# A two-layer hybrid trunk whose instruction order comes from a list scheduler: the same work placed by the finer of its two machine models

## The chip, the cores and the metric

One core of one Trainium2 chip runs the whole program in one launch. The metric is device time in microseconds (us): median of the runs, lower is better. Each of the core's engines works through its own list of instructions in the order in which the list stands: PE (matmul, with its weight loads shown apart as PEld), DVE, ACT and POOL (elementwise work) and SP (issues the DMAs). Engines wait for each other by semaphores. The order of every list is fixed when the program is built, and that order is all that this case changes.

## The reference, cut to what matters

Two layers over 1024 latent tokens and 256 context tokens, 1024 features, all in fp32:

```python
for l in range(DEPTH):                                    # DEPTH = 2
    h_lat = rms_norm(x, g_attn_pre[l]) * (1 + sc1) + sh1   # sh, sc, gt: 6 vectors from adaln(c)
    h_ctx = rms_norm(ctx, g_attn_pre[l]) * (1 + csc1) + csh1
    y_lat, y_ctx = hybrid_mixer(h_lat, h_ctx, ...)
    x = x + gt1 * rms_norm(y_lat, g_attn_post[l])
    h = rms_norm(x, g_mlp_pre[l]) * (1 + sc2) + sh2
    x = x + gt2 * rms_norm(square(relu(h @ w1)) @ w2, g_mlp_post[l])
    ...                                                    # the same for ctx, but in the last layer

def hybrid_mixer(h_lat, h_ctx, ...):
    p = h @ w_in                        # ONE projection, 24 tiles of 128 columns
    # 4 heads of gated DeltaNet: chunks of tokens, a triangular solve in each chunk,
    # then a scan over the chunks, forwards and backwards: S <- S * g + k^T (u - w S)
    # RG-LRU: gates, then a linear recurrence over the tokens, both directions
    # latent attention: 4 heads, keys and queries from small latents, softmax(q k^T) v
    return concat([gdn, rglru, mla]) @ w_out
```

## The kernel before, in words

Activations lie feature-major, 128 features on the partitions and tokens along the row; the tokens are three blocks, "c" (256) and two latent blocks of 512. A large product runs in three passes over operands split into a high and a low part (`mm3`, L222): for each of 8 feature tiles, two matmuls with the high weights `wh` and one with the low weights `wl`. So a tile of 128 output features and 512 tokens is 24 matmuls of 512 columns. The elementwise helpers put nearly all their instructions on four lines: L134 (ACT), L137 (two-operand work on DVE or POOL), L142/L143 (one operand) and L146 (DVE).

In each layer comes first the mixer, then the output projection, then the MLP. The mixer has four kinds of work, and the whole case turns on how they lie beside each other:

- **Projections.** The 24 tiles of `w_in`, each with an evacuation from PSUM and, for most, a short convolution (L146 on DVE) and an activation.
- **Heads.** Four DeltaNet heads (`gdn_head`), one after the other, since the large tiles of a head (`kT`, `qT`, `vt`, `N0`, `at0`, `C`, `X`, ...) have one buffer each. A head is a chain: decays and products of its chunks (L606, L618, L628), the triangular solve, which begins with 30 steps of two DVE instructions (`T<-X`, `X<-X,T`, L137, called from `gdn_invert`) and goes on with small matmuls (L678), then the scan: 10 steps in each direction, and in each step a matmul from the state (L748), one with the inverse (L752), one into the next state (L762) and the outputs (L771, L772), with a DVE or ACT instruction between one and the next. At the end come the norm and transposes of its output (L803).
- **RG-LRU.** 20 segments (`segment` in `lru`): four small matmuls (L830), some ten ACT, ten DVE and nine POOL instructions each, on tiles called `lr`.
- **Attention.** For each of 4 heads a preparation (L934, L942, the maxima L968, L974, L981) and the attention itself (scores L998 to L1000, exponentials on ACT, products with the values L1013). The steps of the adaLN vectors (L258) are mixed into it in layer 0. After it the output projection begins.

In the program's text the order is: the projection tiles of heads 0 to 2, each followed by its head; the two RG-LRU inputs; the tiles of head 3 and head 3; the attention's latents; then RG-LRU and attention. RG-LRU and attention take the memory of the projection's input (`close(self.ap)`), so they can't start before the projections have ended.

Nobody writes the order of the engines by hand. Tile's list scheduler runs the program through a model of the machine in time. Whenever an engine of the model can take an instruction, it gets the one of highest priority (earliest in the program's text, but for a few shifted by `later`) among those whose inputs and buffers are there in the model's time. What the model believes of durations and queues therefore decides which instruction is ready when, and that decides the order that the chip then keeps to.

Of the kernel before, what the change touches and what calls it, by code (L numbers as in the profile page):

```python
# [17 lines left out]
D = 1024  # L18
# [10 lines left out]
# token blocks in the joined order [context | latent]: (start, length)  # L29
# [4 lines left out]
# columns of the per-layer table of small parameters  # L34
# [9 lines left out]
class Trunk:  # L44
# [35 lines left out]
    @contextmanager  # L80
    def actor(self, name, t, g):
        """scratch of its own for a stream of work that runs beside others: t = (pool, buffers), g = PSUM tags."""
        old, self.cur = self.cur, (name, t, g)
        yield
        self.cur = old

    @contextmanager
    def later(self, n=0):
        """work beside what follows it: it takes no place in the order of the engines, and stands n steps later in it"""
# [6 lines left out]
    def T(self, half=None):  # L96
        name, (pool, bufs), _ = self.cur
        if name == "s":
            # two tags, so that a phase can keep two streams apart
            self.ht = 1 - self.ht if half is None else half  # L100
            name, bufs = "s%d" % self.ht, bufs // 2
# [22 lines left out]
    def M4(self, n):  # L124
        """PSUM for the products of a phase that leaves most banks free"""
# [22 lines left out]
    def split(self, dst, src, eng=None):  # L148
        """dst[:, 0] + dst[:, 1] = src, each part of few enough bits for one pass."""
# [12 lines left out]
    def softplus(self, out, x, tmp):  # L162
        """out = max(x, 0) + log1p(exp(-|x|)); tmp(): scratch of x's shape."""
# [15 lines left out]
    def rstd_bc(self, s, n, dim, eps=EPS):  # L179
        """s [128, n] (to be summed over partitions) -> PSUM [128, n]: rsqrt(sum / dim + eps) on every partition."""  # L180
# [13 lines left out]
    def sqsum(self, s, x, first, eng=None):  # L194
        """s (+)= x * x"""
# [20 lines left out]
    def mm3(self, ps, w, acts, ks):  # L216
        """ps = sum over ks of w[k]^T @ acts, in three passes of the split operands."""
# [17 lines left out]
    def ada_mods(self, L, v):  # L235
        """the vector v of (shift, scale, gate) x 2 is there: the products with the gains"""
# [8 lines left out]
    def ada_pe(self, L, vs, pool, tag, bufs, ptag):  # L245
        """one or two vectors of the modulation of a layer, for both streams, by TensorE: a list of steps"""
# [31 lines left out]
    def ada_steps(self, L, vs):  # L278
        """other vectors of the modulation, by VectorE, a quarter of a vector at a time: a list of steps"""
# [27 lines left out]
    def tick(self, n):  # L307
        """n steps of the work that is spread between the weights"""
# [9 lines left out]
    def prenorm(self, b, xs, s, L, which):  # L318
        """xs: 8 fp32 [128, n], s: sum of their squares (None: already normalised) -> 8 split tiles of the
        modulated norm; overwrites xs"""  # L320
# [19 lines left out]
    def fetch(self, src, b, pool, tag, bufs):  # L340
        """x of a block, two feature tiles in one buffer -> 8 tiles"""
# [8 lines left out]
    def post(self, b, ys, s, L, which, xs, xdst, want_sq=True):  # L350
        """ys <- x + gate * norm(ys); written to xdst; returns the sum of squares of the new x."""
# [30 lines left out]
    def conv_tile(self, L, hs, i, col, blocks, done, bias=None):  # L382
        """one projected tile -> depthwise convolution over each segment -> done(block, result)."""
# [22 lines left out]
    def silu2(self, acc):  # L406
        """acc <- 2 silu(acc)"""
# [5 lines left out]
    def qk_tile(self, L, hs, i, ct, blocks, name, tok=False):  # L413
        """-> 2 silu(conv), feature-major (and token-major), and the sums of its squares, a column for each chunk"""
# [20 lines left out]
    def v_tile(self, L, hs, i, ct, blocks, name):  # L435
        """values, token-major"""
# [14 lines left out]
    def z_tile(self, L, hs, i, blocks, d):  # L451
        """silu(z) times the gain of the head norm"""
# [9 lines left out]
    def gelu_tile(self, L, hs, i, blocks, d):  # L462

        def evac(b, ps):
            # gelu(g) = g (1 + tanh(sqrt(2/pi) (g + 0.044715 g^3))) / 2
# [15 lines left out]
    def kv_tile(self, L, hs, i, name):  # L481
        """normalised key/value latents"""
# [12 lines left out]
    def cq_tiles(self, L, hs, i, blocks, name):  # L495
        """normalised query latents: two tiles with one norm"""
# [26 lines left out]
    def gdn_coeffs(self, L, ba):  # L523
        """ba [128, NCH, 16] token-major -> decay and beta columns."""
# [48 lines left out]
    def gdn_head(self, L, h, kss, qss, vd, last):  # L573
        """The keys stay without their l2 norm 1 / rho: with D = diag(rho), the triangular system is solved as
# [815 lines left out]
```

## Time and profile before

| | |
|---|---|
| runs (us) | 3942.18, 3945.51, 3947.01: median 3945.51 |
| span of the profiled execution | 3934.6 us |
| that execution's own time | not listed apart; the median run is 10.9 us above the span |
| PE busy | 3567.8 us, 91% |
| DVE, ACT, POOL busy | 57%, 38%, 30% |
| mean granted PE clock | 0.948 |

Times below are microseconds from the start of the span. By the trace layer 0's mixer lasts to about 1009, its output projection and MLP to about 2190, layer 1's mixer from there to 3039, and the rest is its output projection and MLP. A row of a stretch (as "237.00:366.00") gives for PE, PEld, DVE, ACT and POOL the busy time and, in brackets, the number of instructions, then the granted PE clock (1.00 is full), the share of the DMA engines and their GB/s. PE counts as busy from a matmul's start to its modelled end, and matmuls overlap, so a PE that is busy all the time need not be at its peak. An fp32 matmul that isn't split is two records in the trace and one instruction in the program.

### The profile page before, as it was taken

To read this page: it belongs to the slowest core of one execution; us is meant where nothing else is said; L and a number is where in the kernel's file an instruction comes from. 1 tells how busy PE (TensorE), PEld (TensorE's weight loads), DVE (VectorE), ACT (ScalarE), POOL (GpSimd) and SP (SyncE) were. 2 spreads that over 40 slices of the span, in tenths; PEclk is the share of its full clock that TensorE was granted. 3 is DMA by queue.
4 is the path that set the end of the run, shared out by engine and by line. 5 is a ranking of instruction groups with operands and counts; after the bars stand their busy time and mean duration, and the time that the engine had idled before them with its cause. 6 is when DMAs were issued, how large, how long until landed. Compare 5 with 4: busy or idle time off the path is not lost. (4 is left out here: it accounts for less than half of the span.)

```text
span 3934.6 us, 51412 instructions
## 1 busy us (share of the span) xinstructions
PE 3567.8 (91%) x19396; PEld 2757.3 (70%) x19396; DVE 2231.4 (57%) x4519; ACT 1488.7 (38%) x3269; POOL 1170.3 (30%) x863
## 2 busy tenths in 40 slices
PE   5999898898989999999996798989888989999997
PEld 3777786344667888888885677776445768778775
DVE  6667756667265454545437678677675363333334
ACT  3555454455354211111223455454455432111222
POOL 4211221345463111111126311212255742212223
PEclk9999999898989999999997899999799989999998
DMA  5221222232433222222133222222012432111113
GB/s 179 93 80 63 89 86 74 91 92 81 147 115 102 70 76 70 75 75 69 55 99 100 86 68 83 79 92 68 24 40 90 130 99 70 43 49 48 48 44 123
DMA packets 158009, 321.44 MB, mean 82 GB/s; under 512 B 14784, under 2 KB 73536, under 8 KB 157760
## 3 DMA queue, kind: packets, MB, share of 16 engines
q1 hardware_dynamic: 157760, 318.16, 25.4%
q8 instruction: 152, 2.49, 0.3%
q14 instruction: 97, 0.79, 0.1%
HBM read 252.30 MB, written 65.80 MB: 81 GB/s over the span
## 5 line engine op out<-in xcount | busy, mean ns | idle before, releaser
L137 POOL TENSOR_TENSOR wl<-wr,wh 128x1024 fp32r<-128x1024 f32 x224 | 546.3, 2439 | 1897.3 <-ACT wh L134 1801.0
L222 PE MATMUL mm<-A,wh 128*128 128x512 f32 (+1 forms) x3008 | 898.9, 380 | 29.0 <-ACT T L134 14.7
L222 PEld LDWEIGHTS mm<-A,wh 128*128 128x128 f32 x3008 | 552.6, 195 | 123.4 <-ACT T L134 14.9
L134 ACT ACTIVATE wh<-wr 128x1024 fp32r<-128x1024 f32 x240 | 254.1, 1059 | 968.5 <-PE mm L222 572.5
L222 PE MATMUL mm<-A,wl 128*128 128x512 f32 (+1 forms) x1504 | 569.5, 379 | 7.9 <-POOL wl L137 6.1
L137 DVE TENSOR_TENSOR T<-T 128x256 f32<-128x256 f32 (+1 forms) x160 | 211.4, 1322 | 371.1 <-ACT T L134 371.1
L222 PE MATMUL mm<-hid,wh 128*128 128x512 f32 (+1 forms) x1280 | 376.6, 377 | 7.2 <-DVE acc L137 7.2
L222 PEld LDWEIGHTS mm<-A,wl 128*128 128x128 f32 x1504 | 293.4, 195 | 56.9 <-POOL wl L137 8.4
L222 PEld LDWEIGHTS mm<-hid,wh 128*128 128x128 f32 x1280 | 234.3, 190 | 54.2 <-DVE acc L137 7.4
L222 PE MATMUL mm<-hid,wl 128*128 128x512 f32 (+1 forms) x640 | 240.9, 376 | 0.7 <-POOL wl L137 0.5
L222 PE MATMUL pd<-A,wh 128*128 128x512 f32 (+1 forms) x704 | 238.9, 411 | 1.0 <-issue 0.7
L222 PE MATMUL plr<-A,wh 128*128 128x512 f32 (+1 forms) x800 | 236.5, 379 | 0.0
L222 PE MATMUL pb<-A,wh 128*128 128x512 f32 (+1 forms) x800 | 235.3, 377 | 0.0
L146 DVE SCALAR_TENSOR_TENSOR T<-raw,sm,T 128x512 f32<-128x512 f32 (+4 forms) x240 | 185.5, 775 | 48.5 <-ACT raw L134 26.2
L222 PE MATMUL plr<-hid,wh 128*128 128x512 f32 (+1 forms) x640 | 191.8, 383 | 10.8 <-DVE acc L137 5.0
L137 DVE TENSOR_TENSOR acc<-acc,mm 128x512 f32<-128x512 f32 (+1 forms) x140 | 88.3, 632 | 191.9 <-PE mm L222 191.9
L222 PE MATMUL pb<-hid,wh 128*128 128x512 f32 (+1 forms) x640 | 188.4, 379 | 7.8 <-DVE acc L137 7.8
L134 ACT ACTIVATE hid<-T 128x256 fp32r<-128x256 f32 (+1 forms) x160 | 94.2, 589 | 242.2 <-DVE T L137 242.0
L137 POOL TENSOR_TENSOR S<-S,T 128x512 f32<-128x512 f32 (+1 forms) x126 | 158.0, 1255 | 64.6 <-ACT T L134 59.8
L1013 PE MATMUL pd<-Pt,V 128*128 128x512 f32 (+1 forms) x336 | 168.4, 622 | 8.4 <-ACT Pt L134 4.8
L146 DVE SCALAR_TENSOR_TENSOR ada<-wa,sil,ada 128x256 f32<-128x256 f32 x392 | 165.8, 482 | 8.7 <-DMA wa<-in_w_ada_dram 8.6
L222 PEld LDWEIGHTS plr<-A,wh 128*128 128x128 f32 x800 | 147.6, 192 | 30.1 <-issue 0.5
(369 smaller groups left out, 7138.7 us busy)
## 6 DMA issues: line engine op xcount, KB each, us to landing
wr<-in_w_mlp_dram SPq DMA_DIRECT2D x152, 512.0 KB, 3.6
wa<-in_w_ada_dram SPq DMA_DIRECT2D x96, 512.0 KB, 3.8
wr<-in_w_in_dram SPq DMA_DIRECT2D x48, 512.0 KB, 3.6
wr<-in_w_out_dram SPq DMA_DIRECT2D x40, 512.0 KB, 3.7
A<-y SPq DMA_DIRECT2D x32, 256.0 KB, 3.4
xm<-acc SPq DMA_DIRECT2D x32, 256.0 KB, 2.9
x<-xm SPq DMA_DIRECT2D x16, 512.0 KB, 8.0
kT<-k SPq DMA_DIRECT2D x8, 640.0 KB, 4.2
```

Source lines behind the costliest of these rows:

```text
L134: return self.nc.scalar.activation(out, in_, f, **kw)
L137: return (eng or self.nc.vector).tensor_tensor(out, a, b, op=op)
L146: return self.nc.vector.scalar_tensor_tensor(out, a, s, b, op0=op0, op1=op1)
L222: nc.tensor.matmul(ps, w[wi][:, wk, :], a[:, ai, :], start=n == 0, stop=n == last)
L1013: nc.tensor.matmul(po, V[:, c, :], p, start=ci == 0, stop=ci == len(chunks) - 1)
```

## The change

One argument of the context that builds the program. The lines of comments and docstrings that the diff also empties produce no instruction (the line numbers stay).

```diff
-    with tile.TileContext(nc) as tc, ExitStack() as es:
+    with tile.TileContext(nc, schedule_with_timeline_sim=True) as tc, ExitStack() as es:
```

By default the scheduler's machine is a coarse one. With this argument it is a finer model, which follows queues, semaphores and engines in time. The instructions stay the same ones, engine by engine: 16296 matmuls on PE, 4521 instructions on DVE, 3047 on ACT, 868 on POOL, 902 on SP in both programs, with the same tiles. Only their order differs, and with it where semaphore waits stand.

**PE, the scan of head 0 in layer 0.** Names: `X`, `kT`, `N`, `C`, `at`, `qT`, `Qg` are tiles of head 0; `mm` and `pd` are PSUM tiles of the projections, `A` their input, `wh` and `wl` their weights. Before:

```order
L762 MATMUL pa_1676<-X_266_1648,C_1645 128x128
L772 MATMUL pc_1679<-X_266_1648,at_231_1233 128x128
L752 MATMUL pb_1686<-X_266_1648,N_230_1232 128x128
L222 MATMUL mm_2432<-A_458,wl_2398 128x512
L748 MATMUL pa_1697<-X_266_1648,kT_1224 128x128
L771 MATMUL pc_1693<-X_266_1648,Qg_233_1235 128x128
L222 MATMUL mm_2432<-A_462,wh_2397 128x512
L762 MATMUL pb_1690<-X_266_1648,C_1645 128x128
```

After, from the same L748 on:

```order
L748 MATMUL pa_1697<-X_266_1648,kT_1224 128x128
L222 MATMUL mm_3450<-A_438,wh_3420 128x512
L222 MATMUL mm_3450<-A_438,wl_3421 128x512
L222 MATMUL mm_3450<-A_442,wh_3420 128x512 x2
L762 MATMUL pb_1690<-X_266_1648,C_1645 128x128
L771 MATMUL pc_1693<-X_266_1648,Qg_233_1235 128x128
L772 MATMUL pc_1693<-X_266_1648,at_232_1234 128x128
L222 MATMUL mm_3450<-A_442,wl_3421 128x512
L222 MATMUL mm_3450<-A_446,wh_3420 128x512 x2
L222 MATMUL mm_3450<-A_446,wl_3421 128x512
L222 MATMUL mm_3450<-A_450,wh_3420 128x512 x2
```

Before, one projection matmul stands between two steps of the scan; after, up to twenty. Counted over the whole list from the first L748 of head 0 to its last: 32 projection matmuls of 512 columns and 8 of 256 before, 318 and 150 after in layer 0; 22 and 24 before, 354 and 96 after in layer 1. From the first L748 of head 0 to the first of head 1 there are 235 and 120 before, 677 and 336 after (layer 1: 234 and 72 before, 657 and 144 after). From the first L748 of head 1 to the last of head 3 there are 517 and 240 before (layer 1: 504 and 96); after, 25 of 512 columns in layer 0 and none in layer 1. So nearly all projections now stand ahead of the scan of head 1.

**PE, the start of RG-LRU in layer 0.** Before, its matmuls L830 stand in the scan of head 3 and then all through the attention:

```order
L942 MATMUL pst_6828<-cqn_6746,wq_6791 128x512 x2
L830 MATMUL plr_7001<-lr_6999,lw_6729 64x256 x4
L803 MATMUL pa_6253<-cst,X_5947 128x128 x2
L803 MATMUL pb_6260<-cst,X_5947 128x128 x2
L830 MATMUL plr_7038<-lr_7036,lw_6729 64x256
L803 MATMUL pb_6260<-cst,X_5947 128x128 x2
```

After, they stand in the scan of head 1 (whose tiles are `X_469`, `kT_2516`):

```order
L772 MATMUL pc_3097<-X_469_2940,at_435_2526 128x128
L830 MATMUL plr_7038<-lr_7036,lw_6729 64x256 x4
L185 MATMUL pst_6695<-ones,T_6689 128x1 x4
L748 MATMUL pb_3115<-X_469_2940,kT_2516 128x128
L762 MATMUL pa_3108<-X_469_2940,C_2937 128x128
L771 MATMUL pc_3111<-X_469_2940,qT_2517 128x128
```

All 80 L830 of a layer moved from beside the attention to beside heads 1 and 2. After the last L803 of head 3 there stood 71 of them in layer 0 and 67 in layer 1, and now none; the rest of what stands there up to the output projection is the same in both programs but for one matmul: nearly all of the attention.

**DVE, the solve of head 2 in layer 0.** `X_3940` and `T_3989` are the solve's tiles, `T_48..` and `raw` those of a projection's convolution, `lr` those of RG-LRU. Before:

```order
L137 TENSOR_TENSOR T_3989<-X_3940 128x168
L146 SCALAR_TENSOR_TENSOR T_4864<-raw_4773,sm_84,T_4864 128x512
L137 TENSOR_TENSOR X_3940<-X_3940,T_3989 128x24x7
L146 SCALAR_TENSOR_TENSOR T_4870<-raw_4773,sm_84,T_4870 128x512
L137 TENSOR_TENSOR T_3989<-X_3940 128x184
L146 SCALAR_TENSOR_TENSOR T_4870<-raw_4773,sm_84,T_4870 128x512
```

After:

```order
L137 TENSOR_TENSOR T_3989<-X_3940 128x168
L137 TENSOR_TENSOR X_3940<-X_3940,T_3989 128x24x7
L146 SCALAR_TENSOR_TENSOR lr_7341<-lr_7342,lr_7341 128x256
L137 TENSOR_TENSOR T_3989<-X_3940 128x184
L146 SCALAR_TENSOR_TENSOR lr_7332<-lr_7341,lr_7332 128x256
L846 TENSOR_SCALAR lr_7382<-lr_7381 128x256
```

What stood between the solve's steps was the convolutions of projections (12 instructions); now it is RG-LRU (43 instructions). Between the steps of head 3's solve, where 29 other instructions stood, there are now none.

## The prediction

> **What bounds the kernel now.** I read the page's totals first, then its slices, then the busy time of the engines by stretches of the mixers.
>
> ```profile
> span 3934.6 us, 51412 instructions
> PE 3567.8 (91%) x19396; PEld 2757.3 (70%) x19396; DVE 2231.4 (57%) x4519; ACT 1488.7 (38%) x3269; POOL 1170.3 (30%) x863
> ...
> PE   5999898898989999999996798989888989999997
> ```
>
> PE is busy 91% of the span, and idle for 367 us. That looks as if little could be won or lost. The next rows say otherwise. They are the stretches from one head's scan to the next one's in both layers (237 is the first L748 of head 0, 366, 495 and 641 those of heads 1 to 3; 698 the last L803 of head 3; 1009 the first matmul of the output projection; layer 1 from 2340 likewise), and two for comparison.
>
> ```profile
> 237.00:366.00 129.00, 118.98 (x1007) 99.79 (x1008) 92.88 (x238) 72.10 (x215) 22.36 (x13) 0.97 0.26 87
> 366.00:495.00 129.00, 114.30 (x964) 95.57 (x962) 90.43 (x203) 61.18 (x169) 32.14 (x25) 0.93 0.20 68
> 495.00:641.00 146.00, 136.09 (x1094) 114.16 (x1094) 94.36 (x281) 68.09 (x208) 22.16 (x15) 0.96 0.23 75
> 641.00:698.00 57.00, 43.74 (x247) 31.55 (x247) 32.26 (x99) 36.57 (x112) 18.90 (x23) 0.87 0.27 92
> 698.00:1009.00 311.00, 283.08 (x967) 140.61 (x964) 199.80 (x362) 157.35 (x337) 124.83 (x159) 0.94 0.29 87
> 2340.00:2466.00 126.00, 113.21 (x935) 92.62 (x934) 92.64 (x225) 64.79 (x190) 21.96 (x11) 0.95 0.25 81
> ...
> 2715.00:2773.00 58.00, 43.17 (x222) 31.12 (x222) 35.24 (x101) 33.64 (x101) 22.00 (x27) 0.82 0.15 46
> 2773.00:3039.00 266.00, 237.81 (x790) 128.20 (x791) 180.34 (x314) 140.28 (x295) 114.85 (x145) 0.89 0.15 45
> 735.00:860.00 125.00, 124.70 (x431) 57.01 (x429) 75.94 (x147) 57.26 (x121) 40.28 (x53) 1.00 0.29 88
> 1300.00:1400.00 100.00, 100.00 (x522) 84.65 (x521) 50.49 (x94) 19.68 (x31) 15.64 (x8) 1.00 0.23 69
> ```
>
> In the MLP (1300 to 1400) PE is saturated, and no order makes it shorter. The mixers are different: four heads at one per 126 to 146 us, then 311 and 266 us in which attention and RG-LRU share all engines. A head is a chain of dependent steps, and it doesn't need PE for long; the projections are what fills PE in that time. To price PE's part I need the time from one start to the next, which is shorter than the time that a row calls busy:
>
> ```profile
> 983.26 0.40 PE L999 MATMUL mm<-Q,K 96*128 96x512 f32 x1
> 983.49 0.40 PE L1000 MATMUL mm<-Q,K 96*128 96x512 f32 x1
> ...
> 985.76 0.19 PEld L1013 LDWEIGHTS pd<-Pt,V 128*128 128x128 f32 x1 [0.24 <-issue]
> 986.19 0.19 PEld L1013 LDWEIGHTS pd<-Pt,V 128*128 128x128 f32 x1 [0.24 <-issue]
> ...
> 239.39 0.38 PE L762 MATMUL pa<-X,C 128*128 128x128 f32 x2
> 239.61 0.39 PE L772 MATMUL pc<-X,at 128*128 128x128 f32 x2
> ```
>
> A split matmul of 512 columns costs 0.23 us (983.26 to 983.49), one of 256 half that; an fp32 one of 512 columns two records of 0.43 (985.76 to 986.19); an fp32 one of 128 columns 0.22 for its two records (239.39 to 239.61). The sum of these over a piece of the order I call its issue time. From head 0's scan to head 1's it is 112 us of 129: 235 x 0.233 + 120 x 0.116 = 69 for projections, 43 for the head.
>
> **The change, part by part.** No instruction comes or goes, so only waits can change. Four things move, in both layers.
>
> *1. Projections into the scan of head 0.* From the first L748 of head 0 to that of head 1 now stand 677 and 336 projection matmuls instead of 235 and 120: 442 x 0.233 + 216 x 0.116 = 128 us more, with some transposes 250 us of issue time instead of 112. In layer 1: 225 instead of 104. PE keeps its order, so head 1 can't be earlier than this. The share of the time that is issue time was 112/129 = 0.87 here; PE busy at 119 of 129 says that about 0.94 is the most. I take 0.90: 278 us instead of 129, and 250 instead of 126. Bounds: 266 to 288, and 240 to 272 (at layer 1's own 104/126). Ahead of the first L748 stand 15 and 22 us more issue time, at 0.9 17 and 25. So head 1's scan starts at 237 + 17 + 278 = 532 instead of 366, and at 2340 + 25 + 250 = 2615 instead of 2466. What hides that: the projections themselves, which are then done, at 532 and not at 650.
>
> *2. Heads 2 and 3 without projections, head 2 beside RG-LRU.* This is where the cover goes: PE has nothing else there. The chain of a head, from these rows (first start to last start):
>
> ```profile
> L606 PE MATMUL pa<-cst,gv x10: 272/272/323, 568.5 to 576.2; 128*128 128x128 f32 x10
> L748 PE MATMUL pa<-X,kT x18: 275/275/377, 640.5 to 673.4; 128*128 128x128 f32 x18
> L606 PE MATMUL pa<-cst,gv x10: 272/272/323, 2647.7 to 2654.2; 128*128 128x128 f32 x10
> L748 PE MATMUL pa<-X,kT x18: 275/275/583, 2714.0 to 2751.9; 128*128 128x128 f32 x18
> L748 PE MATMUL pa<-X,kT x18: 270/275/377, 236.8 to 265.3; 128*128 128x128 f32 x18
> L606 PE MATMUL pa<-cst,gv x10: 271/273/421, 281.6 to 292.0; 128*128 128x128 f32 x10
> ...
> L137 DVE TENSOR_TENSOR X<-X,T 128x30 f32<-128x30 f32 (+14 forms) x240 | 96.7, 403 | 4.4
> L137 DVE TENSOR_TENSOR T<-X 128x30 f32<-128x30 f32 (+14 forms) x240 | 94.5, 394 | 4.2
> L146 DVE SCALAR_TENSOR_TENSOR lr<-lr,lr 128x256 f32<-128x256 f32 x218 | 108.2, 506 | 98.7 <-POOL lr L137 77.9 <-ACT lr L134 18.0 <-DMA lr<-lg 1.5
> ```
>
> From the first L606 to the first L748 head 3 took 72 us in layer 0 and 66 in layer 1; a scan takes 30; from the scan's end to the next L606 14 pass (267 to 282). A clean head is 66 + 30 + 14 = 110, and 102 if the solve goes at its 30 x (0.40 + 0.39) = 24 us without the 29 and 26 other DVE instructions of those two. For the scan of head 2 to that of head 3 I take 108 (102 to 122, the stretch 2593 to 2715 of before). For head 1 to head 2, RG-LRU lies on the chain: 43 of its DVE instructions in the solve, 43 x 0.5 = 21 us (46 in layer 1), and by the order 122 DVE instructions in head 1's scan instead of 47. I take 135, between 118 (little of it shows) and 150. From head 3's scan to its last L803 48, against 57 and 58 with other work beside it (45 to 58). So head 3 ends at 532 + 135 + 108 + 48 = 823 instead of 698, and at 2615 + 291 = 2906 instead of 2773: 125 and 133 us later.
>
> *3. RG-LRU away from attention.* After head 3 stands the attention as before, without the 71 and 67 L830. Its issue time is 228 instead of 243 us in layer 0, 175 instead of 188 in layer 1. It can't start earlier, since in PE's order it is behind head 3. Before, 243 us of issue took 311 and 188 took 266: 0.78 and 0.71, with RG-LRU's ACT, DVE and POOL work in the way. Without it the nearest row is 735 to 860, where PE is busy all the time at full clock: 107 us of issue in 125, 0.86. That gives 265 and 203, 46 and 63 us less than before. Bounds: 0.95 (240, 184), and the shares of before (294, 246). The output projection starts at 823 + 265 = 1088 instead of 1009, +79, and at 2906 + 203 = 3109 instead of 3039, +70.
>
> *4. The rest.* Behind the projections of each layer the same matmuls are only interleaved otherwise (2 and 10 of two sums instead of 12 and 12), and in the saturated MLP that costs nothing. Where a norm ends a pass, its small matmuls (L185, L191) stand up to some 50 projection matmuls (11 us) later in PE's order, in the output projections and between the layers. That can shift an idle stretch either way; I take 0, with -10 to +25 in all.
>
> Sum: 79 + 70 = 149 us on the span of 3934.6, so 4084; the median of the runs stands 10.9 above the span of this execution: 4094. The issue times of part 1 alone say why it is not a trade: the work that filled PE beside three heads now fills it beside one, which needs no more than it had.
>
> **The rule that bears on it.** Where PE has little to do, its granted clock falls:
>
> ```profile
> 2770.00:2800.00 30.00, 23.34 (x51) 9.82 (x51) 20.45 (x40) 12.64 (x30) 12.98 (x19) 0.56 0.12 40
> ...
> L803 PE MATMUL pc<-cst,X x4: 270/272/415, 282.7 to 283.8; 128*128 128x128 f32 x4
> L803 PE MATMUL pc<-cst,X x4: 417/417/417, 696.6 to 697.3; 128*128 128x128 f32 x4
> ```
>
> Behind head 3 the clock is 0.56, and the same transpose takes 417 ns instead of 272. The Trainium skill ("TensorE: Matmul & The Clock Gate", Part 1) says that PE runs at half clock after an idle window of about 3.4 us and gets its full clock back after as long a busy one. By that rule heads 2 and 3 would start each piece of PE work slowly, since the solve leaves PE idle; the rows agree so far as they go.
>
> **The rivals.**
>
> *The clock drops all through heads 2 and 3.* Head 3 of layer 1 shows it: its scan took 42 us (2714 to 2756) instead of 30, at a clock of 0.82. Four scans at +11: +44, so 4138. Against it: scans ran at 1.00 where projections were thin too, and there was RG-LRU in that scan as well. [...]
>
> *The queue behind a waiting step.* A scan step in the middle of projections holds the projections behind it, if its DVE or ACT input is late. Part 1 then runs below the 0.87 of before; at 0.78, as in the attention of before, 250 and 225 us take 321 and 288: +81 on the sum, 4175. Against it: between two dependent steps now stand 1 to 5 us of matmuls, longer than the DVE or ACT instruction between them (0.35 us).
>
> *Faster: PE never lacks work.* With its lists this deep, PE could run at its issue time in part 1 and part 3 (250 + 228 and 225 + 175 us). That alone gives 28 + 37 + 25 + 28 = 118 back and leaves +31. It decides only if head 1 to head 3 also go at their lower bounds, 265 instead of 291 in each layer: -21, 3925. For it: the MLP's 100 of 100. Against it: no stretch of a mixer came above 0.94.
>
> *The change does nothing that counts.* If the scheduler moved only work with slack. Against it: head 1's scan is put behind 128 us more matmuls on the engine that is busy 91%, and no row shows such slack.
>
> **How the numbers follow.** Within 0.2% (8 us) a measurement of this kernel can't tell a change from none. The forecast with its own bounds, about 4020 to 4150, gets 0.68; the clock 0.08; the queue 0.08; faster 0.11; no change 0.05. So slower 0.84, same 0.05, faster 0.11. The range takes in the bounds of the three priced parts one or two at a time, the clock and part of the queue: 3980 to 4180; below it lie faster and no change, 0.16.
>
> **What would show it.** In the profile after: the first L748 of head 1 near 532 and 2615; the scans of head 0 some 125 us long instead of 30, with PE busy above 90% around them; from about 560 to 820 and 2640 to 2900 PE busy about half, at a lower clock; no L830 after that, and the attention 265 and 203 us long; the MLP as before. I am wrong in part 1 if head 1 starts much before 500, in part 2 if a head takes 80 us without projections, in part 3 if the attention without RG-LRU still takes 311 us, or far less than 240.

## The result, and the profile after

| | before | after |
|---|---|---|
| median of the runs beside each other (us) | 3943.85 | 4276.88 (4272.19 to 4283.92) |
| ratio, 95% interval | | 1.086 (1.084 to 1.088) |
| span of the profiled execution | 3934.6 | 4276.9 |
| PE busy | 3567.8, 91% | 3631.6, 85% |
| mean granted PE clock | 0.948 | 0.893 |

The change costs 333 us, or 342 between the two profiled spans. The forecast was +149, with a range that ended at 4180. The sign was right, the size was not.

From the page of the kernel after: span, PE's totals, PE in 40 slices and the granted clock in the same slices.

```profile
span 4276.9 us, 51340 instructions
PE 3631.6 (85%) x19396; PEld 2834.8 (66%) x19396; DVE 2306.1 (54%) x4519; ACT 1487.0 (35%) x3269; POOL 1193.9 (28%) x863
...
PE   6999845588897999999994899864587978999997
...
PEclk9999966788898999999996899976778888999998
```

There are two new holes, slices 6 to 8 and 27 to 29, one in each mixer, where the heads are. In them PE is about half idle, at 0.6 to 0.7 of its clock. Before, PE read 8 or 9 there. (The single 4 in slice 22 lies between the layers, where PE read 6 before.) The same stretches as in the prediction, now at the places where the heads' scans begin (columns as there; 1450 to 1550 lies in the MLP):

```profile
237.00:499.00 262.00, 251.44 (x1717) 215.14 (x1717) 155.27 (x348) 119.68 (x332) 52.66 (x33) 0.97 0.24 80
499.00:690.00 191.00, 105.53 (x839) 73.70 (x838) 157.17 (x374) 115.65 (x312) 126.65 (x153) 0.67 0.25 80
690.00:804.00 114.00, 64.07 (x624) 52.87 (x623) 68.78 (x189) 42.74 (x134) 21.78 (x25) 0.65 0.14 47
804.00:843.00 39.00, 30.69 (x193) 25.38 (x192) 16.80 (x59) 20.65 (x76) 0.00 (x0) 0.90 0.04 11
843.00:1162.00 319.00, 265.58 (x825) 139.99 (x826) 134.64 (x203) 90.30 (x174) 25.77 (x21) 0.84 0.19 62
2538.00:2783.00 245.00, 230.64 (x1536) 192.46 (x1535) 154.67 (x362) 125.03 (x332) 66.27 (x51) 0.95 0.28 91
2783.00:2960.00 177.00, 93.96 (x748) 64.69 (x747) 148.53 (x340) 100.25 (x267) 117.68 (x142) 0.63 0.21 67
2960.00:3060.00 100.00, 54.34 (x602) 45.64 (x601) 59.77 (x165) 34.70 (x109) 7.82 (x6) 0.70 0.11 39
3060.00:3097.00 37.00, 28.72 (x176) 23.36 (x175) 16.02 (x56) 18.31 (x65) 0.00 (x0) 0.92 0.03 8
3097.00:3378.00 281.00, 230.33 (x661) 131.89 (x660) 120.10 (x166) 80.12 (x142) 22.16 (x15) 0.80 0.07 21
1450.00:1550.00 100.00, 100.00 (x525) 84.84 (x525) 52.21 (x104) 22.36 (x36) 15.06 (x7) 1.00 0.26 80
```

Beside the rows of before and the forecast (us; s0 to s3 are the first L748 of heads 0 to 3, y the last L803, o the first matmul of the output projection):

| stretch | layer 0: before, forecast, after | layer 1: before, forecast, after |
|---|---|---|
| s0 to s1 | 129, 278, 263 | 126, 250, 244 |
| s1 to s2 | 129, 135, **190** | 126, 135, **177** |
| s2 to s3 | 146, 108, 115 | 121, 108, 100 |
| s3 to y | 57, 48, 39 | 59, 48, 38 |
| y to o, the attention | 312, 265, **319** | 266, 203, **280** |
| o to s0 of layer 1; o to the end | 1331, 1356, 1376 | 896, 896, 899 |

(Another 17 us had been forecast ahead of s0 in layer 0.) Two rows carry the miss. The attention should have become 46 and 63 us shorter without the RG-LRU beside it, and became 8 and 14 longer. The head with the RG-LRU beside it took 190 and 177 instead of 135. The experiments are about these two, and about whether the projections are the cause of the rest.

### The profile page after: what moved, and what is told of

Read it like the earlier page. It is cut to its first block, busy times and chain, and to the rows that moved or that the text cites. A ratio compares the mean times of both kernels' runs of the same rounds, so it can differ in the third digit from the quotient of the medians.

```text
span 4276.9 us, 51340 instructions
## 1 busy us (share of the span) xinstructions
PE 3631.6 (85%) x19396; PEld 2834.8 (66%) x19396; DVE 2306.1 (54%) x4519; ACT 1487.0 (35%) x3269; POOL 1193.9 (28%) x863
## 4 chain that ended last, share of the span: by engine, by line
PE 68%; DVE 18%; ACT 4%; issue 3%; POOL 2%; DMA 2%; SPq 0%; POOLq 0%; DVEq 0%; ACTq 0%
PE mm L222 27%; PE plr L222 10%; PE pb L222 10%; PE pd L222 4%; PE pd L1013 4%; DVE T L137 3%; DVE X L137 2%; DVE acc L137 1%; DVE T L146 1%; DVE n4s L137 1%; DVE lr L146 1%; ACT T L134 1%; DVE acc L146 1%; DVE mx L969 1%; DVE T L1015 1%
## 5 line engine op out<-in xcount | busy, mean ns | idle before, releaser
L222 PE MATMUL mm<-A,wh 128*128 128x512 f32 (+1 forms) x3008 | 877.2, 375 | 39.3 <-ACT A L134 20.3
L222 PE MATMUL mm<-A,wl 128*128 128x512 f32 (+1 forms) x1504 | 559.2, 372 | 6.0 <-DVE wl L137 5.7
L222 PE MATMUL pd<-A,wh 128*128 128x512 f32 (+1 forms) x704 | 225.5, 399 | 1.1 <-ACT T L134 0.5
L137 POOL TENSOR_TENSOR Q<-T,Q 32x512 fp32r<-32x512 f32 (+1 forms) x20 | 24.3, 1221 | 591.2 <-ACT Q L134 533.1
L1013 PE MATMUL pd<-Pt,V 128*128 128x512 f32 (+1 forms) x336 | 168.4, 650 | 3.9 <-DVE T L137 3.8
```

Of the source, the lines that this page charges most:

```text
L137: return (eng or self.nc.vector).tensor_tensor(out, a, b, op=op)
L222: nc.tensor.matmul(ps, w[wi][:, wk, :], a[:, ai, :], start=n == 0, stop=n == last)
L1013: nc.tensor.matmul(po, V[:, c, :], p, start=ci == 0, stop=ci == len(chunks) - 1)
```

## The experiments

A tool for the first three: Tile can open a *block*, which its scheduler places by itself, by the coarse or the finer model, and which nothing leaves or enters. With the heads in one block and the attention in another, each can have its own model. Differences below are from medians of runs beside the same kernel before, 3936 to 3938 us.

**Control: two blocks a layer, both coarse.**

```diff
+        blk = self.tc.block(schedule_with_timeline_sim=False)
+        blk.__enter__()
         for h in range(3):
             tiles(h)
             head(h)
...
         kvq()
+        blk.__exit__(None, None, None)
         self.close(self.ap)
+        blk = self.tc.block(schedule_with_timeline_sim=False)
+        blk.__enter__()
...
         load(7)
+        blk.__exit__(None, None, None)
```

> Control: the kernel before, with the four heads of a layer in a block of their own and the attention in another, both placed by the coarse model; a block is scheduled by itself and nothing crosses its ends. All theories: head to head 129/129/146 us in layer 0 and the attention 311, 266 us as before; the four ends of blocks cost 0 to 15 us each, so 3945 to 4000 us.

Measured: 4037 us, 1.026 (1.024 to 1.027). The heads are as expected (125, 133 and 151 us in layer 0). The attention to the output projection takes 372 and 312 us instead of 312 and 266: the ends of a block cost more than I took, since nothing of the preparation or of the output projection crosses them. In layer 0 PE sits idle for 12.1 us at the start of that stretch until the input of the keys has come by DMA, and for 18.1 us at its end until ACT has split the first weight of the output projection. So only differences to this control count.

**Finer model in the attention's block alone** (the second `False` becomes `True`).

> As the control, but the attention's block (with the RG-LRU in it) is placed by the finer model. Theory A (the finer model's own order inside the attention is what costs, not only the RG-LRU's leaving): the attention takes 345 to 390 us in layer 0 and 300 to 340 in layer 1 where the control has about 311 and 266, and the kernel is 60 to 150 us slower than the control. Rival (the order inside the attention costs nothing; the stretch did not shrink because its own chains and the lower clock bound it whatever else runs beside): the attention stays within 15 us of the control's in each layer and the time within 1%.

The control's two attentions, then this kernel's:

```profile
700.00:1071.00 371.00, 303.68 (x1000) 147.61 (x1000) 218.00 (x385) 172.11 (x369) 145.24 (x180) 0.88 0.31 96
2825.00:3137.00 312.00, 249.43 (x825) 135.28 (x825) 200.32 (x347) 158.43 (x336) 136.66 (x171) 0.86 0.18 55
```

```profile
702.00:1104.00 402.00, 306.81 (x1001) 157.89 (x1000) 218.77 (x385) 172.87 (x370) 147.59 (x180) 0.81 0.29 89
2861.00:3211.00 350.00, 264.12 (x826) 142.74 (x825) 208.76 (x347) 161.30 (x337) 142.73 (x170) 0.79 0.16 49
```

Measured: 4116 us, 79 more than the control, of it 31 and 38 us in the two attentions. The same instructions in the finer model's order are slower, at a lower clock. Theory A holds. Its absolute figures missed, by the cost of the block.

**Finer model in the heads' block alone** (the first `False` becomes `True`).

> As the control, but the heads' block is placed by the finer model; the RG-LRU cannot leave the attention's block, so no head has it beside it. Theory B (the RG-LRU lengthens the passage from head 1's to head 2's scan): scan 0 to 1 about 262 and 245 us as in the changed kernel, scan 1 to 2 falls from 191 and 177 to 110 to 130, scan 2 to 3 about 114 and 100, attention about 311 and 266; 60 to 75 us a layer more than the control in the heads and up to 45 between the layers, so 4060 to 4150 us. Rival (head 1 takes 190 us with no projections beside it because of the low clock alone): scan 1 to 2 stays at 170 to 195 and the kernel is 250 to 300 us slower than the control.

Heads 0, 1 and 2 of layer 0 and head 1 of layer 1, scan to scan:

```profile
268.00:513.00 245.00, 240.94 (x1685) 206.63 (x1685) 152.12 (x353) 115.00 (x319) 50.15 (x33) 1.00 0.24 80
513.00:623.00 110.00, 57.55 (x650) 49.90 (x650) 68.86 (x206) 40.05 (x129) 11.79 (x10) 0.72 0.15 50
623.00:731.00 108.00, 57.53 (x621) 48.96 (x620) 61.76 (x170) 37.99 (x123) 10.36 (x10) 0.69 0.11 37
2738.00:2841.00 103.00, 57.69 (x598) 48.36 (x597) 60.29 (x168) 34.32 (x107) 7.81 (x6) 0.64 0.10 35
```

Measured: 4194 us, 157 more than the control. The first head takes 245 us with all projections in it, the others 102 to 109 with none; in layer 1 the first takes 224. The low clock (0.64 to 0.72) does not keep them from that: the rival falls, and theory B stands. (Scan 0 to 1 is 17 and 21 us shorter than expected; the time and the attentions lie above the expectation, as the control's do.) The four heads take 502 us instead of 452 in layer 0 and 468 instead of 415 in layer 1; another 21 and 33 us pass ahead of head 0's scan.

**No RG-LRU, coarse model.** The loop over the segments becomes a copy of the gate:

```diff
-        def segment(d, t, b):
-           ...
+        for t in range(2):
+            for b in range(5):
+                cs = slice(b * W, (b + 1) * W)
+                if cs.start >= y0:
+                    q = R()
+                    nc.sync.dma_start(q, gd[t][:, cs])
+                    nc.sync.dma_start(yd[t][:, cs], q)
```

> The kernel before with the RG-LRU's arithmetic left out (its two output tiles are filled with the gate instead), all else placed by the coarse model: the attention by the coarse order without the RG-LRU. Theory A: what the prediction took, 240 to 290 us in layer 0 and 184 to 240 in layer 1. Rival: the attention's own chains bound it, and it takes 300 us or more and 255 or more, as with the RG-LRU.

```profile
682.00:944.00 262.00, 254.75 (x826) 128.45 (x826) 132.25 (x204) 91.29 (x173) 24.77 (x22) 0.92 0.24 75
2703.00:2906.00 203.00, 192.48 (x657) 112.17 (x657) 117.51 (x166) 79.72 (x141) 18.22 (x14) 0.94 0.09 28
```

Measured: 3809 us (one run). The attention takes 262 and 203 us; the forecast had 265 and 203. So that term was right for the coarse order, and wrong for the order that the changed kernel has.

**No RG-LRU, finer model** (the same edit in the changed kernel).

> The changed kernel with the RG-LRU's arithmetic left out (its two output tiles are filled with the gate instead). Theory B (the RG-LRU beside heads 1 and 2 is what makes scan 1 to 2 take 190 and 177 us): those two fall to 104 to 115, the rest of the heads stays as in the changed kernel. Theory A: the attention stays at 319 and 280 us (within 8), since the RG-LRU was not beside it; against 262 and 202 in the coarse order without it. Together about 4277 - 150 = 4127 us. Rival to B (the low clock and the missing projections make the passage long): it stays above 165 in both layers. Rival to A (something left of the RG-LRU slowed the attention): it falls below 290 and 245.

The passage from head 1's to head 2's scan in both layers, then the two attentions:

```profile
497.50:628.50 131.00, 76.23 (x685) 61.95 (x684) 76.24 (x223) 48.25 (x144) 21.13 (x20) 0.69 0.27 85
2707.30:2818.30 111.00, 60.94 (x609) 49.76 (x607) 68.93 (x181) 38.37 (x115) 14.29 (x11) 0.67 0.13 45
771.50:1091.60 320.10, 266.82 (x828) 140.74 (x827) 135.57 (x203) 91.52 (x174) 26.37 (x21) 0.83 0.20 62
2958.10:3233.20 275.10, 225.02 (x658) 128.88 (x658) 120.79 (x166) 80.47 (x142) 22.07 (x15) 0.83 0.07 21
```

Measured: 4133 us (one run). The RG-LRU beside the head costs 59 and 66 us (190 to 131, 177 to 111); layer 0 stays above the expected 115, with 25 projection matmuls still in it. The attention stays at 320 and 275, against 262 and 203 for the same work in the coarse order. Both theories hold.

**Projections tied to the heads, finer model.** One column of a raw weight takes a zero times a value of an earlier head's scan, so its tile can't be projected before:

```diff
             nc.sync.dma_start(raw, ap)
+            if self.gate is not None:
+                self.stt(raw[:, 0:1], self.gate, 0.0, raw[:, 0:1], ALU.mult, ALU.add)
...
                 o = self.gdn_head(L, h, *kd[h], last)
+                go = self.small([P, 1], "go", 8)
+                nc.vector.tensor_copy(go, o[:, 2, 0:1])
+                gates.append(go)
...
         for h in range(3):
+            self.gate = gates[h - 2] if h >= 2 else None
             tiles(h)
             head(h)
+        self.gate = gates[1]
         xtile(0)
...
+        self.gate = gates[2]
         kvq()
```

> The changed kernel, finer model, with the projections tied to the heads by data: the weights of head 2's tiles take a zero from head 0's scan, those of the RG-LRU's inputs and head 3 one from head 1's scan, those of the latents one from head 2's (one more DVE instruction a weight tile). So they can't run ahead, and by the order 192 + 96, 353 + 192 and 175 + 72 projection matmuls stand from scan to scan in layer 0 where the changed kernel has 677 + 336, 25 + 0 and none. Theory C (the projections run ahead, and then are missing as cover, is what the heads lose): scan 0 to 1 about 125, 1 to 2 150 to 170, 2 to 3 110 to 145, the four heads with the last output 430 to 500 us in layer 0 against 606 in the changed kernel and 461 before, and 380 to 440 in layer 1 against 559 and 433; 3990 to 4080 us in all. Rival (the finer model orders the inside of a head badly, whatever lies beside it): four heads above 540 and 500, and above 4130 us.

Measured: 4161 us, 224 above the kernel before where the changed kernel is 333 above it; the expectation's range ended at 4080. Scan 0 to 1 takes 139 and 130, scan 1 to 2 166 and 159, scan 2 to 3 169 and 155; the four heads 534 and 509. The second is as theory C has it, the first is a little above its 125, the third is well above. In layer 1 the heads and, in all, the time even lie where the rival had put them (above 500 and above 4130). But the RG-LRU now lies beside heads 2 and 3, which the expectation had left out. So it was tied too:

**Projections and RG-LRU tied, finer model.** The edit above, and

```diff
         nc.sync.dma_start(self.lw, self.I["lru_w"][l])
+        self.stt(self.lw[:, 0, 0, 0, 0:1], gates[3], 0.0, self.lw[:, 0, 0, 0, 0:1], ALU.mult, ALU.add)
```

> The kernel with the projections tied to the heads (finer model), and now also the RG-LRU's weights tied to head 3's scan, so that the RG-LRU stays beside the attention as before. Both moves between the stages are undone; the finer model's order within them is left. Theory (projections, RG-LRU and the attention's own order are three separate costs): scan 2 to 3 falls from 169 and 155 to 115 to 145, the last head's output from 60 and 65 to 40 to 50; the attention with the RG-LRU beside it in the finer order takes 335 to 355 and 290 to 312; 4020 to 4095 us. Rival (what was left in the heads after the projections were tied is the finer order inside a head): scan 2 to 3 stays above 155 and the time above 4130.

Measured: 4118 us, 1.045 (1.043 to 1.047). Scan 2 to 3 falls to 154 and 134, the last output to 42 and 41; the four heads take 500 and 464 us, against 606 and 559 in the changed kernel and 461 and 433 before. The attention takes 358 and 310, 46 and 44 more than before. With both moves undone 153 of the changed kernel's 333 us are gone. The other 180 lie in the attention (90), in the heads (70) and around them. Of the 70 the cause is not shown: the ties are coarser than the coarse model's order, with 545 projection matmuls between scans 1 and 2 of layer 0 instead of 342, but the finer model's own order inside a head may have its part. The sum was expected too low, at 4020 to 4095, and so were scan 2 to 3 in layer 0 (at most 145) and, by 3 us, the attention there.

**The attention's waits.** Four experiments say that the finer order itself is slow there, but not why. This is PE's order in layer 1, one letter a row: k and q keys and queries (L934, L942), m maxima (L968), t their transposition (L974), v values (L981), S scores (L998), P value products (L1013), l RG-LRU (L830). Before, then after:

```
SvtvSvvkPkkPqqPPmPmPmmPmmlmlPmmlSSSSSmSmmSPtmPmmPmPmmlmlPmmSmSmPmPvtPvvvSk
vtvPvSkSSkPPPPqkSSSSSqSmSmmmmPPPPmmPmmmmmmtmmSSSmmSSSmmSSmSmSmmmvtvPvSkSSk
```

After an m, DVE has to take a maximum over 512 columns, 0.69 us, before PE may use that PSUM bank again, and there are two banks. In this layer 31 of 96 rows m were followed by another m before, and 58 of 96 after. The trace of the changed kernel at one of these places (start, duration, engine, line; in brackets the engine's wait):

```profile
3232.71 0.28 PE L968 MATMUL pst<-K,Q 96*128 96x256 f32 x1
3232.91 1.42 DVE L137 TENSOR_TENSOR T<-pb,raw 32x512 f32<-32x512 f32 x2
3234.36 3.36 DVE L1015 RECIPROCAL T<-pd 64x512 f32<-64x512 f32 x1
...
3234.47 0.55 PE L968 MATMUL pb<-K,Q 96*128 96x512 f32 x1 [1.48 <-DVE T L137]
3237.75 0.42 DVE L969 TENSOR_REDUCE mx<-pst 128x1 f32<-128x256 f32 x1
...
3238.23 0.79 PE L968 MATMUL pst<-K,Q 96*128 96x512 f32 x1 [3.21 <-DVE mx L969]
3238.92 0.69 DVE L969 TENSOR_REDUCE mx<-pb 128x1 f32<-128x512 f32 x1
```

The division of the previous head stands on DVE ahead of the maximum that PE needs, for 3.36 us. The matmul after the wait takes 0.79 us instead of the 0.40 of its equals at full clock. Summed over layer 1's attention, what PE waited for, in the changed kernel and then in the coarse order without the RG-LRU (where L968 is L915; us, times, longest):

```profile
PE pb L968 <- DVE mx L969: 23.2, 13, 4.3
PE pst L968 <- DVE mx L969: 11.7, 8, 3.5
```

```profile
PE pb L915 <- DVE mx L916: 4.7, 7, 0.9
...
PE pst L915 <- DVE mx L916: 1.1, 2, 0.8
```

**Short maxima, finer and coarse model** (one edit in both kernels; the order of PE hardly moves in the finer one).

```diff
-                    nc.vector.tensor_reduce(mx[:, i, j:j + 1], pm, axis=AX.X, op=ALU.max)
+                    nc.vector.tensor_reduce(mx[:, i, j:j + 1], pm[:, 0:64], axis=AX.X, op=ALU.max)
...
-        sc = 96.0 ** -0.5
+        sc = 0.02 * 96.0 ** -0.5
```

> The changed kernel with the maxima (DVE, L969) taken over 64 of the 512 columns, so 0.1 to 0.2 us each instead of 0.68; the scale of the scores is made smaller so that the exponentials stay finite. The order of PE in the attention stays nearly the same. Theory D (in the finer model's order the maxima's matmuls stand in a row on two PSUM banks and wait for DVE to empty them, and that is the main part of what the attention loses): attention 280 to 300 in layer 0 and 235 to 255 in layer 1 instead of 319 and 280, 4277 - 60 = about 4215 us, the idle time behind mx at L968 under 8 us in each layer. Rival (it is the lower clock, or the bursts of scores and value products): attention within 10 us of 319 and 280.

> The kernel before with the same shorter maxima and scale. Theory D: the coarse order has scores between the maxima, which cover DVE, so little is won: attention 300 to 312 and 255 to 266, 3920 to 3950 us. Rival (the maxima cost the same in any order): it falls by as much as in the changed kernel.

Measured: the changed kernel 4232 us, its attention 299 and 259, 21 us less in each layer: less than theory D's 60 in all, and the waits for mx do not vanish (16.7 and 8.1 us in layer 1), since the reciprocal still stands in the way. The kernel before does not gain, it loses: 3963 us, 1.006 (1.005 to 1.008), attention 320 and 282, outside both expectations. Its scheduler knows the shorter maxima and places the work in another order, so this is not the same order with less work, and it settles nothing. That the coarse order hardly waits for the maxima is shown by its rows: 5.8 us in layer 1 without the RG-LRU (above), and 7.2 us in the kernel before.

**No reciprocal, then neither, finer model.**

```diff
-            nc.vector.reciprocal(rc, po[64:128, :])
+            nc.vector.tensor_copy(rc, po[64:128, :])
```

> The changed kernel with the reciprocal of the attention's sums (DVE, L1015, 3.36 us for 512 columns, 20 of them) replaced by a copy of the same size (about 0.6 us): the attention's outputs are not divided. PE's order in the attention stays nearly the same. Theory D2 (in the finer model's order the reciprocal stands on DVE ahead of maxima that PE waits for, up to 4.3 us at a time): attention 290 to 300 us in layer 0 and 250 to 260 in layer 1 instead of 319 and 280, about 4225 us, no wait for mx at L968 above 2 us. Rival (the waits only move to the next late thing): attention within 8 us of 319 and 280.

> The changed kernel with both: the short maxima (and the smaller scale) and the copy for the reciprocal. If the waits for DVE at the preparation of the next head are the whole of what the finer order costs the attention, it falls to 262 to 272 and 202 to 215 us, the coarse order's without the RG-LRU, with a granted clock of 0.92 or more, and about 4165 us. If they are only part of it (the preparation's own chain of evacuation, maximum, transposition and negated row, with no scores beside it, is the rest): 275 to 290 and 225 to 245, and the clock stays below 0.90.

Measured: without the reciprocal 4244 us, attention 303 and 261, a little above the expectation, and no wait for mx in layer 1 above 1.9 us. Without both 4201 us, attention 278 and 237:

```profile
841.00:1119.00 278.00, 248.27 (x815) 130.31 (x815) 76.26 (x203) 88.24 (x170) 25.03 (x21) 0.90 0.23 71
3062.00:3299.00 237.00, 215.12 (x655) 124.13 (x656) 66.36 (x166) 78.97 (x141) 20.59 (x15) 0.86 0.08 24
```

The two together give back 41 and 43 of the 58 and 78 us that separate the finer order from the coarse one without RG-LRU. So what these two edits take away is the larger part, not the whole: the second branch of the expectation. Two limits: no run takes both out of the coarse order, so part of the 41 and 43 us may be work saved and not waits, and PE still waits 11.8 us for maxima in layer 1. The last 17 and 35 us stay open; in layer 1 a third of them is idle time (21.9 us against 10.5), the rest busy time at a lower clock (0.86 against 0.94).

**Which part of the RG-LRU slows the head.** In the changed kernel, once its POOL instructions and once its DVE instructions are left out. The scheduler then places the rest again, so some of the RG-LRU moves: between scans 1 and 2 stand 76 and 64 of its matmuls in the changed kernel, 68 and 64 without POOL's part, 80 and 56 without DVE's. In the first kernel, these and all others with `gp` (seven or eight a segment):

```diff
-            self.ts(wh, wh, 1e-30, ALU.max, eng=gp)
-            self.tt(r, wh, r, ALU.mult, gp)
...
```

and, in the second kernel, these and all others of the segment on DVE:

```diff
-            self.stt(u, y, 1.0, u, ALU.add, ALU.mult)
-            self.stt(r, r, 1.0, q, ALU.min, ALU.mult)
...
```

> The changed kernel with the RG-LRU's POOL instructions left out (nine a segment), its ACT and DVE instructions and PE's order as they are. Theory E1 (the RG-LRU's DVE instructions stand between the steps of head 1's scan and head 2's solve, and their time is what is added): scan 1 to 2 stays above 165 and 150 us (190 and 177 in the changed kernel, 131 and 111 without the RG-LRU). Theory E2 (POOL's work at the same time makes DVE's instructions longer; the solve's two steps took 0.51 and 0.47 us beside it and 0.33 without): the solve's steps go back to 0.33 to 0.36 us and the RG-LRU's own from 0.56 to about 0.45, together 15 to 25 us less, 160 to 175 and 150 to 162. Both can hold.

> The changed kernel with the RG-LRU's DVE instructions left out (eight or nine a segment), its ACT, POOL and PE work as it is. Theory E1: scan 1 to 2 falls to 131 to 145 and 111 to 125 us. Theory E2 alone (POOL slows DVE): it falls by less than half of the 59 and 66 us that leaving all of the RG-LRU out gave, to 160 and 145 or more, and the solve's steps stay near 0.5 us. Rival to both (ACT's work of the RG-LRU delays the head's own exponentials and copies): it stays above 160 with the solve's steps at 0.33.

The costliest groups on DVE between scans 1 and 2 of layer 0 (busy us, mean ns of one): the changed kernel, without POOL's part, without DVE's part, without the RG-LRU.

```profile
L146 DVE SCALAR_TENSOR_TENSOR lr<-lr,lr 128x256 f32<-128x256 f32 x98 | 53.0, 561 | 9.7 <-POOL lr L137 6.4 <-ACT lr L134 2.8
L137 DVE TENSOR_TENSOR T<-X 128x30 f32<-128x30 f32 (+14 forms) x30 | 15.2, 508 | 0.4
L137 DVE TENSOR_TENSOR X<-X,T 128x30 f32<-128x30 f32 (+14 forms) x30 | 14.2, 474 | 0.4
...
L146 DVE SCALAR_TENSOR_TENSOR N<-pc,hc,at 128x128 f32<-128x128 f32 x20 | 5.4, 344 | 1.3 <-PE pc L618 1.3
```

```profile
L146 DVE SCALAR_TENSOR_TENSOR lr<-lr,lr 128x256 f32<-128x256 f32 x88 | 41.4, 472 | 8.7 <-ACT lr L134 5.4 <-DMA lr<-lg 2.5
L137 DVE TENSOR_TENSOR X<-X,T 128x30 f32<-128x30 f32 (+14 forms) x30 | 9.8, 326 | 0.3
```

```profile
L137 DVE TENSOR_TENSOR T<-X 128x30 f32<-128x30 f32 (+14 forms) x30 | 17.2, 573 | 1.0
L137 DVE TENSOR_TENSOR X<-X,T 128x30 f32<-128x30 f32 (+14 forms) x30 | 16.2, 539 | 1.0
L146 DVE SCALAR_TENSOR_TENSOR N<-pc,hc,at 128x128 f32<-128x128 f32 x20 | 5.4, 342 | 6.9 <-PE pc L618 4.0 <-ACT lr L134 2.9
```

```profile
L137 DVE TENSOR_TENSOR X<-X,T 128x30 f32<-128x30 f32 (+14 forms) x30 | 10.0, 332 | 1.0
```

Scan 1 to 2 takes 154 and 151 us without POOL's part (4205 us in all) and 172 and 139 without DVE's (4219), against 190 and 177 with both and 131 and 111 with neither. Neither is the whole. POOL's part counts 37 and 26 us, more than E2 took, DVE's 19 and 38, less than E1 took; the two add up to 56 and 64 of the 59 and 66. POOL acts at least in part through DVE: without it the solve's step falls from 0.51 to 0.33 us; without the RG-LRU's DVE work, but with POOL busy 126 of 172 us, it is 0.57, which also speaks against ACT as the cause. In the changed kernel's own trace, of the 60 solve instructions in this stretch of layer 0 the 20 that lay wholly beside POOL work took 0.63 us on average, the 16 with none beside them 0.32. The rows also show where it does not act: `N<-pc,hc,at`, with one input from PSUM, takes 0.34 us whatever POOL does. In layer 0 the longer DVE instructions make up about 18 of POOL's 37 us, and DVE's waits for POOL were 6.4; the rest is not broken down.

**A cheaper RG-LRU on PE, coarse model.** That its removal won 127 us suggested a version that might beat both kernels:

```diff
-                for q in (0, 64):
-                    nc.tensor.matmul(ps[q:q + 64, g, :], self.lw[q:q + 64, d, g, t, :], u[q:q + 64, :], start=True,
-                                     stop=True, tile_position=(q, q))
+                nc.tensor.matmul(ps[:, g, :], self.lw[:, d, g, t, :], u, start=True, stop=True)
```

> The kernel before (coarse model) with the RG-LRU's gates as one matmul of 128 x 128 with a block-diagonal weight in place of two of 64 x 64 on two quarters of the array: 40 instead of 80 of these instructions a layer, the same result. Leaving the RG-LRU out took 28 us of PE's busy time off layer 0's attention and 127 us off the kernel. If PE's share decides and two quarters run one after the other: 10 to 15 us less in each attention, 3905 to 3925 us. If the quarters run at the same time: no change, 3930 to 3945 us.

Measured: 3937 us, 0.999 (0.998 to 1.000): no change. In the trace of the kernel before, the two records of one quarter take 0.64 us, and four records of both quarters 0.65 when they stand together:

```profile
742.82 0.64 PE L830 MATMUL plr<-lr,lw 64*64 64x256 f32 x2
...
779.17 0.65 PE L830 MATMUL plr<-lr,lw 64*64 64x256 f32 x4
```

So the quarters do run beside each other. No version here that does the same work beats the kernel before.

## Why the prediction was wrong, point by point

**Part 1, projections into head 0's scan: right in its mechanism, a little high.** 263 us for 278 (3 below its lower bound) and 244 for 250, at a share of issue time of 0.95 and 0.92 where I took 0.90. The lower bound rested on a misread row: 119 of 129 is 0.92, not 0.94, and neither is the most, as the 0.95 shows. The start of head 0's scan did not move in layer 0 (237), where 17 us were forecast. Head 1's scan starts at 499, at the edge of what I had named as refuting. The heads in a block of their own show 245 and 224 with the attention left as it was.

**Part 2, heads without projections: right; the RG-LRU beside one: mis-sized.** Heads with neither take 100 to 115 us for the forecast 108. Scan 1 to 2 is the term that failed, 135 for 190 and 177: +97 us over both layers. I charged the RG-LRU with 43 DVE instructions at 0.5 us in the solve. Measured, it costs 59 and 66 us: its DVE time in the scan, which I had counted and then priced at little, waits of DVE for POOL, and solve steps that go from 0.33 to 0.51 us. The last was in the trace of before for anyone who asked why the same step took 0.40 and 0.39 us there; I used these durations without asking. Of the 480 solve instructions 463 took 0.33 us on average and 17 took 1.4 to 2.6, each beside a POOL instruction, 13 of them beside the splitting of a weight:

```profile
181.82 2.40 POOL L137 TENSOR_TENSOR wl<-wr,wh 128x1024 fp32r<-128x1024 f32 x1 [5.03 <-ACT wh L134]
...
181.94 2.41 DVE L137 TENSOR_TENSOR T<-X 128x108 f32<-128x108 f32 x1
```

The rule for it is in the Trainium skill ("SBUF — State Buffer", "Who interferes with whom"): a DVE instruction with two inputs in SBUF contends with a POOL instruction that reads SBUF. The trace agrees: of the rows shown, those with two such inputs (the solve's, the RG-LRU's) changed, and `N<-pc,hc,at` did not.

**Part 3, the attention without RG-LRU: the step that failed.** The forecast said "After head 3 stands the attention as before, without the 71 and 67 L830", and priced it by rows of the old order: 265 and 203. In the old order it does take 262 and 203. But the same set of instructions is not the same order: the new one puts the maxima in rows and the division ahead of them, and takes 320 and 275 with no RG-LRU anywhere, which is what the forecast had named as its sign of being wrong here. Measured +8 and +14 instead of -46 and -63, 131 us, two thirds of the miss of 193 between the spans. In layer 1 the 78 us between the two orders are 40 of idle time (50.6 against 10.5) and 38 of busy time at a lower clock: 230.3 us at 0.80 and 192.5 at 0.94 are 184 and 181 at full clock, the same work. Leaving out the long maxima and the division gave back 41 and 43 us; why the rest is lost stays open.

**Part 4, the rest.** +0 was right for the tail (899 for 896) and the MLP (100 of 100 us busy). Between the layers it is +45, where the forecast had 25; the heads in a block of their own show +33 there.

**The rivals.** *The clock drops through heads 2 and 3*: it does (0.63 to 0.70), but the scans of heads 2 and 3 take 26 to 34 us, not 42, so it is not what lengthened the heads. It did cost where I had not looked, in the attention. *The queue behind a waiting step*: no, part 1 ran at 0.92 and more. *PE never lacks work*: it lacks it in both holes. *Nothing that counts*: the time is 1.086 of before.

**The clock rule that was weighed.** The Trainium skill ("TensorE: Matmul & The Clock Gate", Part 1) has half clock after an idle window of about 3.4 us. The trace does not bear this out. At the place shown above the granted clock is halved at 3234.71, before the wait of 3.21 us begins. In the 3.4 us ahead of that PE was busy for 1.9 us, and its longest idle piece was the 1.48 us in front of the matmul at 3234.47:

```profile
3231.30:3234.70 3.40, 1.92 (x9) 1.32 (x7) 2.41 (x4) 1.19 (x2) 0.38 (x1) 1.00 0.00 0
3234.72:3238.22 3.50, 0.30 (x1) 0.00 (x0) 3.44 (x3) 0.00 (x0) 0.00 (x0) 0.50 0.00 0
```

In this trace the clock is 1.00 or 0.50, and it falls 62 times. In the 3.41 us ahead of a fall PE was busy 68% of the time at most, and its longest idle piece was between 0.7 and 3.4 us. So several short waits were enough here, and the matmul's 0.79 us is not the price of the one long wait.

## What to carry to other kernels

When a scheduler places the whole program anew, compare the order inside each stage, not only what moved between stages: a stage with the same instructions can lose more than the moved work gives back. Ask of each row of dependent instructions what stands between two of them on the engine that waits and what stands ahead of their producer on its engine, and price the longest instruction there (here a reciprocal of 3.36 us) as a wait. Cover is worth keeping even at the price of some delay: in the block runs the four heads of layer 0 took 452 us with projections beside all of them and 502 with all projections beside the first.

## What the runs showed of the hardware

- POOL slows DVE where both read SBUF: the same DVE instruction took 0.33 us with POOL idle and 0.51 to 0.57 on average with it busy, and 2.4 us when it began beside a POOL instruction of 2.4 us; one with an input from PSUM stayed at 0.34.
- A DVE reciprocal of 64 x 512 takes 3.36 us, five times a multiplication of that size (0.68). The finer model let it stand ahead of work that PE waits for.
- 64 x 64 matmuls on two quarters of the array ran side by side: four records in 0.65 us, two in 0.64. One 128 x 128 matmul in place of two did not shorten the kernel.
- PE's granted clock fell to half at 3234.71 of the changed kernel, when its longest idle piece in the 3.4 us before had been 1.48 us.
- Four blocks of the scheduler cost 100 us at their ends, nearly all of it between the last head and the output projection.
